# The last block pair of each FFN: left half of the down columns plain and joined with the lone block, right half by seven products

## The chip, the cores and the metric

The kernel runs on one core of one Trainium2 chip. The metric is the device time of one execution in microseconds (us). Before the change it is 2223.72 us, the median of three runs (2223.66 to 2224.74).

## The reference, cut to what matters

Two layers. Each has a mixer (not touched by the change) and ends with a SwiGLU FFN; the residual stream has 256 tokens of 2048 numbers, the FFN's hidden width is 5632, and everything is float32:

```python
        x = x + rms_norm(mix, g[1])
        h = rms_norm(x, g[2])
        f = (jax.nn.silu(h @ ffn_w_gate[layer]) * (h @ ffn_w_up[layer])) @ ffn_w_down[layer]
        x = x + rms_norm(f, g[3])
```

## The kernel before, in words

**Tiles.** The 256 tokens are two tiles of 128 (`t` = 0, 1). The hidden width is cut into 11 blocks of 512, the output width 2048 into 4 column blocks of 512 (`n` = 0 to 3). Weights come from memory in halves of 128x1024 numbers (512 KB). Every half is split into a rounded part `whi` (one copy on ACT, line 184) and a rest `wlo` (one subtraction on DVE, line 186), both kept in pools of seven buffers. A product with one 128x512 weight piece is three matmuls: high by `whi`, high by `wlo`, low by `whi` (lines 211 to 213 in `unit_a`, lines 618 to 620 in `quads`). A plain down product of one hidden block, one token tile and one column block is 4 pieces, so 12 matmuls.

**FFN.** `gate_up(b, ...)` makes the gate and up products of hidden block `b` by `unit_a` (8 chunks, 192 matmuls), forms `h` on DVE (line 466) out of the two accumulators and transposes it on PE (line 285, tile `tp`). Blocks 0 to 9 go in five pairs. After a pair, `combos` makes seven left operands `so` of the four transposed `h` tiles (ACT copy, DVE subtraction, and DVE sums), and `quads` runs as a generator in the background of the next pair's `gate_up`: for the left columns (`p` = 0: n = 0, 1) and then the right ones (`p` = 1: n = 2, 3) it makes the product of 2 hidden blocks, 2 token tiles and 2 column blocks by seven products in place of eight (84 matmuls in place of 96). The price is on DVE: 8 additions of weight halves (line 567, `sw<-sw,sw`), 14 splits in place of 8, and 10 additions of a product into the output sums `f` and a helper sum `fu` (line 627). Weights of `quads` come over a stream of their own into tiles `sw` (line 523).

**The lone block.** Block 10 has no pair. During its `gate_up` the quads of the last pair (blocks 8 and 9) run in the background: `tick` after every part of a unit adds `0.5 * rate` to a credit, and each whole credit advances the generator by one step; the rate is 1.0 in the pairs and 2.0 here. A quad has four steps of settling (once per pair) and 14 steps. What is left after the lone block's `gate_up` is run at once; then `fu` is added to or taken from `f` (lines 508 and 510), and `post` makes the lone block's own down products (one chunk of 12 matmuls per `n` and `t`, operands `hth`, `htl`), the norm of `f`, and the residual sum into `x`. `post` begins by loading the residual `x` again from memory (`load_x`, line 635, four transfers of 512 KB on POOL's queue) and the gains `gb` (line 371), before any of its products.

**Order.** The instruction order on each engine is made by a list scheduler from priorities; the engines then run their queues in order. In the FFN `tight` makes `unit_a` alternate the two token tiles; without it, the second token tile's parts lag by up to four (`push`). `wstream` and `sstream` (both on SP's queue) are packed in the order in which the program asks for weights.

Of the kernel before, what the change touches and what calls it, by code (L numbers as in the profile page):

```python
# [18 lines left out]
F32 = mybir.dt.float32  # L19
F32R = mybir.dt.float32r  # L20
# [6 lines left out]
P = 128  # L27
# [64 lines left out]
class Trunk:  # L92
# [102 lines left out]
        while self.pending:  # L195
            self.pending.popleft()()

    def unit_a(self, chunks, xk, evac):

        nc = self.nc  # L200
        last = len(chunks) - 1
        ps = {}

        def part(t, ci, w, kt0, half):
            if ci == 0 and half == 0:
                ps[t] = self.pacc.tile([P, 512], F32, tag="acc", name=self.nm("acc"))
            for k in (2 * half, 2 * half + 1):
                wh, wl = w[half]
                xh, xl = xk(kt0 + k, t)
                s, e = ci == 0 and k == 0, ci == last and k == 3  # L210
                self.pin(nc.tensor.matmul(ps[t], xh, wh[:, k % 2], start=s, stop=False))  # L211
                self.pin(nc.tensor.matmul(ps[t], xh, wl[:, k % 2], start=False, stop=False))  # L212
                self.pin(nc.tensor.matmul(ps[t], xl, wh[:, k % 2], start=False, stop=e))  # L213
# [132 lines left out]
        nc.vector.tensor_copy(row, ps)  # L346
        return row

    def post(self, li, gi, nseg, after, f=None):


        nc = self.nc
# [4 lines left out]
        rs = [self.small([P, 1], "prs", "prs") for _ in range(2)]  # L357
        state = {"si": 0}

        def seg(mk, xk):  # L360
            si = state["si"]
            state["si"] += 1
            last = si == nseg - 1
            if last:
                self.x = [[None, None], [None, None]]
                for t in range(2):
                    for j in range(2):
                        self.load_x(t, j, nc.gpsimd)
# [48 lines left out]
            for n in range(4):  # L417
                def evac(t, ps, n=n):
                    if not last:
                        return add(t, ps, n)  # L420
                    if n == 3 and t == 0:
                        self.prep()
                        self.pinning = ("PE", "DVE")
                    with self.tc.high_priority(offset=NORM):
                        d = add(t, ps, n, n == 3)
                        self.sumsq(d, ssp[t][:, n:n + 1])
                        if n == 3:
                            self.rstd(ssp[t], 4, D, rs[t])
                        i = (nc.gpsimd if n < 3 or (t and MULP and not (li == 1 and gi == 3)) else nc.vector).tensor_mul(out=d, in0=d, in1=gb[n])
                        if n == 3:  # L430
                            self.pin(i)
                    if n == 3 and t == 0:
                        self.pinning = ("PE",)
                        self.pending.popleft()()
                        self.pending.popleft()()
                        self.pinning = ("PE", "DVE")
                if last and n == 2:
                    self.pinned = {}
                    self.pinning = ("PE",)
                self.unit_a(mk(n), xk, evac)  # L440
            if last:
                run(PROG[0])
                assert not self.pending
# [8 lines left out]
    def ffn(self, li, norm, after):  # L452
        nc = self.nc
# [18 lines left out]
        f = [[self.slot([P, 1024], nm="f") for _ in range(2)] for _ in range(2)] + [self.slot([P, 1024], nm="fu")]  # L472
        self.rate, self.width = 1.0, 1
        for pi, pair in enumerate(PAIRS):
            self.squeue.extend((li, b, n) for p in range(2) for b, n in (
                (pair[0], 2 * p), (pair[0], 2 * p + 1), (pair[1], 2 * p + 1), (pair[1], 2 * p)))
        for pi, pair in enumerate(PAIRS):
            h = {}
# [10 lines left out]
            self.flush()  # L489
            while self.bg:  # L490
                self.step()
            self.spawn(self.quads(li, pair, self.combos(h), f, pi == 0))
        ht = self.new_xt(1, "ht")

        def whole(t, tp):
            sl = slice(t * P, (t + 1) * P)
            self.split(tp, ht[0][0][:, :, sl], ht[1][0][:, :, sl])
        self.rate = 2.0
        gate_up(LONE, whole)
        while self.bg:  # L500
            self.step()
        for n in range(4):
            u = f[2][:, n // 2 * 512:n // 2 * 512 + 512]
            c = slice(n % 2 * 512, n % 2 * 512 + 512)
            for t in range(2):
                d = f[t][n // 2][:, c]
                if n % 2 == 0 and t:
                    nc.vector.tensor_add(d, d, u)
                if n % 2:
                    nc.vector.tensor_sub(d, d, u)  # L510
        self.tight = False
        seg = self.post(li, 3, 1, after, f[:2])
        seg(lambda n: [("ffn_w_down", li, 512 * LONE, 512 * n, 0)], self.xk(ht))

    def sload(self):

# [8 lines left out]
        self.splan.append(("A", "ffn_w_down", li, 512 * b, 512 * n))  # L525
        self.sraw[li, b, n] = tiles

    def combos(self, h):

        nc = self.nc  # L530
        out = {}

        def put(key, src):
            o = self.slot([P, 2, 4, P], F32R, "so")
            nc.scalar.copy(o[:, 0], src)
            nc.vector.tensor_sub(o[:, 1], src, o[:, 0].bitcast(F32))  # L536
            out[key] = o
        put("b11", h[0, 0])
        put("b21", h[0, 1])
        put("t4", h[1, 1])  # L540
# [14 lines left out]
    def quads(self, li, pair, ops, f, first):  # L555

        nc = self.nc
        for _ in range(SETTLE):
            yield
        for p in range(2):  # L560
            n0, n1 = 2 * p, 2 * p + 1
            raw = {}

# [45 lines left out]
            for key in order:  # L609
                ps = self.mx([P, 512], "sq")  # L610
                x = ops[key]
                for i in range(2):
                    next(ahead, None)
                    wh, wl = (v.rearrange("p (k n) -> p k n", k=2) for v in ready.popleft())
                    for k in range(2):
                        s, e = i == 0 and k == 0, i == 1 and k == 1
                        xh, xl = x[:, 0, 2 * i + k], x[:, 1, 2 * i + k]
                        nc.tensor.matmul(ps, xh, wh[:, k], start=s, stop=False)  # L618
                        nc.tensor.matmul(ps, xh, wl[:, k], start=False, stop=False)  # L619
                        nc.tensor.matmul(ps, xl, wh[:, k], start=False, stop=e)  # L620
# [790 lines left out]
```

## Time and profile before

| what | value |
|---|---|
| median of three runs | 2223.72 us |
| the profiled execution | 2221.77 us |
| its span, first to last instruction | 2220.0 us |
| PE busy | 2173.3 us (98%) |
| PE weight loads busy | 1829.0 us (82%) |
| DVE busy | 1772.4 us (80%) |
| ACT busy | 1213.5 us (55%) |
| mean granted TensorE clock | 0.992 |

The profiled execution took 1.77 us more than its span and 1.95 us less than the median. Each row of the profile's groups gives a line, an engine, an operation with its output and inputs, the count, the busy time and the mean duration in ns. Matmuls overlap in PE's pipeline, so a row's duration of 0.39 us is longer than the distance between two starts; where PE's pace is wanted, starts are compared.

### The profile page before, as it was taken

Reading aid. Unit: us, or ns where it says so; the run is one execution under the profiler, and the core shown is the slowest. Engines: PE = TensorE matmul, PEld = TensorE weight load, DVE = VectorE, ACT = ScalarE, POOL = GpSimd, SP = SyncE. Lnnn points to the kernel's source line nnn. Section 1 sums busy time; section 2 is a strip of 40 time slices with the busy share of each in tenths; the row PEclk is TensorE's granted clock in tenths of the full one; section 3 lists DMA queues with packets and bytes.
Section 4 is the critical chain, followed back from the end, with each engine's and each line's share of the span. In section 5 each row is a group of like instructions: output and inputs, shape, how many; then the busy total and the mean of one; then the engine's idle time right before and its main releaser. Section 6 shows DMA issues by size and latency. Waiting matters only on the chain.

```text
span 2220.0 us, 28963 instructions
## 1 busy us (share of the span) xinstructions
PE 2173.3 (98%) x10840; PEld 1829.0 (82%) x10840; DVE 1772.4 (80%) x2137; ACT 1213.5 (55%) x1515; POOL 205.3 (9%) x246
## 2 busy tenths in 40 slices
PE   8999999999999999999989999999999999999997
PEld 7989998788888888888768988878888888888875
DVE  7987545766878898888989988676687889888896
ACT  7544435555565555555656545655555555555563
POOL 0001010210000000000021362121000000000002
PEclk9999999999999999999999999999999999999998
DMA  8445565574665555465556443657466555646563
GB/s 282 133 133 184 182 203 182 180 258 157 204 234 189 204 178 201 159 217 199 204 188 223 158 144 114 224 187 260 158 201 229 198 204 170 202 165 209 199 216 116
DMA packets 117325, 424.54 MB, mean 191 GB/s; under 512 B 13392, under 2 KB 13520, under 8 KB 117184
## 3 DMA queue, kind: packets, MB, share of 16 engines
q1 hardware_dynamic: 110592, 400.61, 53.6%
q0 software_dynamic: 6448, 21.99, 3.0%
q8 instruction: 85, 1.39, 0.2%
q14 instruction: 56, 0.46, 0.1%
q10 hardware_dynamic: 144, 0.10, 0.0%
HBM read 414.25 MB, written 8.39 MB: 190 GB/s over the span
## 4 chain that ended last, share of the span: by engine, by line
PE 86%; DVE 10%; issue 2%; POOL 1%; DMA 1%; ACT 0%; DVEq 0%; POOLq 0%; ACTq 0%
PE acc L213 19%; PE acc L212 19%; PE acc L211 19%; DVE wlo L186 5%; PE sq L618 5%; PE sq L619 5%; PE sq L620 5%; PE accb L242 3%; PE accb L244 3%; PE accb L243 3%; PE tp L285 1%; DVE sw L567 1%; DVE xtl L331 1%; DVE f L627 1%; PE gs L819 1%
## 5 line engine op out<-in xcount | busy, mean ns | idle before, releaser
L186 DVE TENSOR_TENSOR wlo<-raw,whi 128x1024 fp32r<-128x1024 f32 x596 | 740.0, 1249 | 278.0 <-ACT whi L184 270.7
L184 ACT CAST whi<-raw 128x1024 fp32r<-128x1024 f32 x596 | 624.7, 1052 | 572.1 <-PE acc L213 388.7
L213 PE MATMUL acc<-whi,xtl 128*128 128x512 f32 x1760 | 689.7, 393 | 5.9 <-DVE xtl L331 5.9
L212 PE MATMUL acc<-wlo,xth 128*128 128x512 f32 x1760 | 689.3, 393 | 0.8 <-DVE wlo L186 0.8
L211 PE MATMUL acc<-whi,xth 128*128 128x512 f32 x1760 | 677.4, 393 | 3.1 <-ACT xth L328 3.0
L184 ACT CAST whi<-sw 128x1024 fp32r<-128x1024 f32 x280 | 293.7, 1054 | 232.0 <-PE acc L213 131.0
L213 PEld LDWEIGHTS acc<-whi,xtl 128*128 128x128 f32 x1760 | 332.4, 189 | 78.1 <-DVE xtl L331 9.3
L211 PEld LDWEIGHTS acc<-whi,xth 128*128 128x128 f32 x1760 | 332.3, 189 | 73.0 <-ACT xth L328 5.1
L212 PEld LDWEIGHTS acc<-wlo,xth 128*128 128x128 f32 x1760 | 332.4, 189 | 70.4 <-DVE wlo L186 1.7
L186 DVE TENSOR_TENSOR wlo<-sw,whi 128x1024 fp32r<-128x1024 f32 x280 | 338.2, 1222 | 48.9 <-ACT whi L184 46.0
L619 PE MATMUL sq<-wlo,so 128*128 128x512 f32 x560 | 220.0, 393 | 4.5 <-DVE wlo L186 4.5
L620 PE MATMUL sq<-whi,so 128*128 128x512 f32 x560 | 219.4, 392 | 0.0
L618 PE MATMUL sq<-whi,so 128*128 128x512 f32 x560 | 219.0, 393 | 0.0
L567 DVE TENSOR_TENSOR sw<-sw,sw 128x1024 f32<-128x1024 f32 x160 | 194.1, 1221 | 16.8 <-DMA sw<-sstream 16.3
L242 PE MATMUL accb<-xth,whi 128*128 128x256 f32 x608 | 173.8, 286 | 0.0
L244 PE MATMUL accb<-xth,wlo 128*128 128x256 f32 x608 | 173.0, 284 | 0.0
L243 PE MATMUL accb<-xtl,whi 128*128 128x256 f32 x608 | 172.7, 284 | 0.0
L619 PEld LDWEIGHTS sq<-wlo,so 128*128 128x128 f32 x560 | 105.9, 189 | 28.5 <-DVE wlo L186 7.0
L620 PEld LDWEIGHTS sq<-whi,so 128*128 128x128 f32 x560 | 106.0, 189 | 22.5 <-DVE so L536 0.6
L618 PEld LDWEIGHTS sq<-whi,so 128*128 128x128 f32 x560 | 105.8, 189 | 22.1 <-ACT whi L184 0.4
L635 POOL DMA_DIRECT2D x<-xm x8 | 4.4, 546 | 1292.5 <-ACT whi L184 645.6
L242 PEld LDWEIGHTS accb<-xth,whi 128*128 128x128 f32 x608 | 116.5, 192 | 1.4 <-issue 0.7
(248 smaller groups left out, 2226.9 us busy)
## 6 DMA issues: line engine op xcount, KB each, us to landing
raw<-wstream SPq DMA_DIRECT2D x596, 512.0 KB, 4.9
sw<-sstream SPq DMA_DIRECT2D x160, 512.0 KB, 6.2
gb<-norm_gains POOLq DMA_DIRECT2D x16, 256.0 KB, 7.6
xm<-x POOLq DMA_DIRECT2D x16, 256.0 KB, 3.5
x<-xm POOLq DMA_DIRECT2D x8, 512.0 KB, 5.1
x<-x SPq DMA_DIRECT2D x4, 512.0 KB, 8.2
x<-x POOLq DMA_DIRECT2D x4, 512.0 KB, 7.8
xf<-x POOLq DMA_DIRECT2D x8, 256.0 KB, 3.4
```

Source lines behind the costliest of these rows:

```text
L184: self.pin(nc.scalar.copy(hi, src))
L186: self.pin(nc.vector.tensor_sub(lo, src, hi.bitcast(F32)))
L211: self.pin(nc.tensor.matmul(ps[t], xh, wh[:, k % 2], start=s, stop=False))
L212: self.pin(nc.tensor.matmul(ps[t], xh, wl[:, k % 2], start=False, stop=False))
L213: self.pin(nc.tensor.matmul(ps[t], xl, wh[:, k % 2], start=False, stop=e))
L242: nc.tensor.matmul(ps, wh[:, kt % 8], xh, start=kt == 0, stop=False)
L243: nc.tensor.matmul(ps, wh[:, kt % 8], xl, start=False, stop=False)
L244: nc.tensor.matmul(ps, wl[:, kt % 8], xh, start=False, stop=kt == 15)
L567: nc.vector.tensor_add(a, a, b)
L618: nc.tensor.matmul(ps, xh, wh[:, k], start=s, stop=False)
L619: nc.tensor.matmul(ps, xh, wl[:, k], start=False, stop=False)
L620: nc.tensor.matmul(ps, xl, wh[:, k], start=False, stop=e)
```

## The change

The last pair's left columns leave `quads` (`COLS`). Their products go into `unit_a` together with the lone block's: for n = 0 and 1 a unit has three chunks (blocks 8, 9 and 10), for n = 2 and 3 one. The pair's operands come from `combos`, which already has three of the four plain ones (`b11`, `b21`, `t4`) and now makes the fourth, `a21`, for this pair. The background rate during the lone block is 0.75 in place of 2.0, so that the remaining quad runs on into the units n = 0 and 1 and is drained ahead of n = 2. These two units are tight, but for the last chunk of n = 1. The helper sum `fu` is taken in at n = 0 for the left columns and at n = 2 for the right ones, and the residual `x` is loaded at n = 2.

```diff
-NCHUNK = 298
-NQUAD = 80
+COLS = [(0, 1)] * 4 + [(1,)]
+NCHUNK = 306
+NQUAD = 72
+ENDRATE = .75
...
-            if self.tight:
+            if self.tight and (loose is None or ci < loose):
...
+        def reload():
+            self.x = [[None, None], [None, None]]
+            for t in range(2):
+                for j in range(2):
+                    self.load_x(t, j, nc.gpsimd)
...
             if last:
-                self.x = [[None, None], [None, None]]
-                for t in range(2):
-                    for j in range(2):
-                        self.load_x(t, j, nc.gpsimd)
+                if before is None:
+                    reload()
...
+                if before is not None:
+                    before(n)
+                    if n == 2:
+                        reload()
...
-                self.unit_a(mk(n), xk, evac)
+                self.unit_a(mk(n), xk, evac, len(mk(n)) - 1 if n == 1 else None)
...
-            self.spawn(self.quads(li, pair, self.combos(h), f, pi == 0))
+            ops = self.combos(h, pi == len(PAIRS) - 1)
+            self.spawn(self.quads(li, pair, COLS[pi], ops, f, pi == 0))
...
-        self.rate = 2.0
+        def before(n):
+
+            if n == 2:
+                while self.bg:
+                    self.step()
+                self.tight = False
+            if n % 2 == 0:
+                u = f[2][:, n // 2 * 512:n // 2 * 512 + 512]
+                left, right = ([f[t][n // 2][:, c * 512:c * 512 + 512] for t in range(2)] for c in range(2))
+                nc.vector.tensor_add(left[1], left[1], u)
+                for d in right:
+                    nc.vector.tensor_sub(d, d, u)
+
+        def operand(kt, t):
+            b, k = kt // 4, kt % 4
+            if b == 2:
+                return self.xk(ht)(k, t)
+            o = ops[(("b11", "a21"), ("b21", "t4"))[b][t]]
+            return o[0][:, k], o[1][:, k]
+        self.rate = ENDRATE
         gate_up(LONE, whole)
-        while self.bg:
-            self.step()
...
-        seg(lambda n: [("ffn_w_down", li, 512 * LONE, 512 * n, 0)], self.xk(ht))
+        own = [(b, 4 * i) for i, b in enumerate((*PAIRS[-1], LONE))]
+        seg(lambda n: [("ffn_w_down", li, 512 * b, 512 * n, k) for b, k in (own[2:] if n > 1 else own)], operand)
...
+        if whole:
+            out["a21"] = self.mtmp([P, 4, P], F32R, "a21"), self.mtmp([P, 4, P], F32R, "a21")
+            part("a21", h[1, 0])
...
-        for p in range(2):
+        for p in cols:
```

Over both layers PE gets 24 instructions more (10522 to 10546), DVE 46 fewer (2139 to 2093) and ACT 10 fewer (1418 to 1408); SP's loads stay 756 in number and alike in size (16 of `sw` become 16 of `raw`).

Three places in the first layer. **PE, at the end of the lone block's up product** (`acc_9373` and `acc_9236` are its last accumulators; `tp` with `h` is the transpose of the lone block's hidden tile; `sq` is the quad). Before:

```order
L211 MATMUL acc_9373<-whi_9610,xth_4217 128x512
L212 MATMUL acc_9373<-wlo_9612,xth_4217 128x512
L213 MATMUL acc_9373<-whi_9610,xtl_4218 128x512
L285 MATMUL tp_9658<-ca,h_9656 128x128 x4
L618 MATMUL sq_9665<-whi_9623,so_9005 128x512
L619 MATMUL sq_9665<-wlo_9625,so_9005 128x512
```

The same place now:

```order
L216 MATMUL acc_9236<-whi_9388,xtl_4218 128x512
L646 MATMUL sq_9404<-whi_9359,so_9020 128x512
...
L214 MATMUL acc_9483<-whi_9473,so_8999 128x512
...
L215 MATMUL acc_9490<-wlo_9475,a_1785_9028 128x512
...
L216 MATMUL acc_9483<-whi_9479,so_8999 128x512
L288 MATMUL tp_9423<-ca,h_9421 128x128 x4
L288 MATMUL tp_9438<-ca,h_9436 128x128 x4
```

The transposes stood right behind the up product's last matmul; now 6 matmuls of the quad and 15 of the pair's plain products (`acc_9483`, `acc_9490`) stand between.

**DVE, at the same point** (`h_9656` and `h_9421` are the lone block's hidden tiles of t = 0). Before:

```order
L627 TENSOR_TENSOR f_4270<-f_4270,sq_9620 128x512
L186 TENSOR_TENSOR wlo_9753<-raw_9608,whi_9751 128x1024
L510 TENSOR_TENSOR f_4272<-f_4272,fu_4273 128x512
L186 TENSOR_TENSOR wlo_9759<-raw_9720,whi_9757 128x1024
L466 SCALAR_TENSOR_TENSOR h_9656<-acc_9359,nrs_4144,sg_9305 128x512
L466 SCALAR_TENSOR_TENSOR h_9678<-acc_9373,nrs_4300,sg_9330 128x512
```

Now:

```order
L188 TENSOR_TENSOR wlo_9475<-raw_9335,whi_9473 128x1024
L188 TENSOR_TENSOR wlo_9481<-raw_9380,whi_9479 128x1024
L188 TENSOR_TENSOR wlo_9506<-sw_9363,whi_9504 128x1024
L477 SCALAR_TENSOR_TENSOR h_9421<-acc_9229,nrs_4144,sg_9195 128x512
L477 SCALAR_TENSOR_TENSOR h_9436<-acc_9236,nrs_4300,sg_9203 128x512
```

From the last pair's last `h` of t = 0 up to and with the lone block's first `h`, DVE's queue held 97 instructions, 59 of 128x1024 and 38 of 128x512; now it holds 52, 32 and 20.

**POOL, the reload of x** (`gb` are the gains, `f_4269` with `gb_9714` or `gb_9462` is the product for n = 1, t = 0, `prs` the norm's factor). Before:

```order
L635 DMA x_9704<-xm_147 128x1024
L635 DMA x_9706<-xm_147 128x1024
L635 DMA x_9708<-xm_148 128x1024
L635 DMA x_9710<-xm_148 128x1024
L371 DMA gb_9712<-norm_gains 128x512
L371 DMA gb_9714<-norm_gains 128x512
L371 DMA gb_9716<-norm_gains 128x512
L371 DMA gb_9718<-norm_gains 128x512
L429 TENSOR_TENSOR f_4269<-f_4269,gb_9712 128x512
L429 TENSOR_TENSOR f_4269<-f_4269,gb_9714 128x512
```

Now:

```order
L378 DMA gb_9464<-norm_gains 128x512
L378 DMA gb_9466<-norm_gains 128x512
L436 TENSOR_TENSOR f_4269<-f_4269,gb_9460 128x512
L436 TENSOR_TENSOR f_4271<-f_4271,gb_9460 128x512
L436 TENSOR_TENSOR f_4269<-f_4269,gb_9462 128x512
L663 DMA x_9755<-xm_147 128x1024
L663 DMA x_9757<-xm_147 128x1024
L663 DMA x_9759<-xm_148 128x1024
L663 DMA x_9761<-xm_148 128x1024
L436 TENSOR_TENSOR f_4270<-f_4270,gb_9464 128x512
L302 TENSOR_TENSOR prs_9458<-ms_9828,mhalf 128x1
```

The four loads of `x` moved behind the gains' loads and three multiplications, to just ahead of the multiplication for n = 2.

More of the change, by code (lines that the diff above doesn't have):

```diff
@@ L347, in rstd_rows, with post @@
         return row
-    def post(self, li, gi, nseg, after, f=None):
+    def post(self, li, gi, nseg, after, f=None, before=None):
         nc = self.nc
@@ L474, in ffn @@
         for pi, pair in enumerate(PAIRS):
-            self.squeue.extend((li, b, n) for p in range(2) for b, n in (
+            self.squeue.extend((li, b, n) for p in COLS[pi] for b, n in (
                 (pair[0], 2 * p), (pair[0], 2 * p + 1), (pair[1], 2 * p + 1), (pair[1], 2 * p)))
@@ L497, in whole @@
             self.split(tp, ht[0][0][:, :, sl], ht[1][0][:, :, sl])
-        self.rate = 2.0
-        gate_up(LONE, whole)
-        while self.bg:
-            self.step()
[L502 to L512, printed above, removed]
-        seg(lambda n: [("ffn_w_down", li, 512 * LONE, 512 * n, 0)], self.xk(ht))
+        def before(n):
[16 more added lines that the diff above has]
+        self.rate = ENDRATE
+        gate_up(LONE, whole)
+        seg = self.post(li, 3, 1, after, f[:2], before)
+        own = [(b, 4 * i) for i, b in enumerate((*PAIRS[-1], LONE))]
+        seg(lambda n: [("ffn_w_down", li, 512 * b, 512 * n, k) for b, k in (own[2:] if n > 1 else own)], operand)
     def sload(self):
@@ L534, in put, with part @@
             o = self.slot([P, 2, 4, P], F32R, "so")
-            nc.scalar.copy(o[:, 0], src)
-            nc.vector.tensor_sub(o[:, 1], src, o[:, 0].bitcast(F32))
-            out[key] = o
+            out[key] = o[:, 0], o[:, 1]
+            part(key, src)
+        def part(key, src):
+            hi, lo = out[key]
+            nc.scalar.copy(hi, src)
+            nc.vector.tensor_sub(lo, src, hi.bitcast(F32))
         put("b11", h[0, 0])
```

8 lines of the change are left out of this document (4 added, 4 removed).

## The prediction

> **What bounds the kernel now.** First the page's first part, the busy time of each engine:
>
> ```profile
> span 2220.0 us, 28963 instructions
> PE 2173.3 (98%) x10840; PEld 1829.0 (82%) x10840; DVE 1772.4 (80%) x2137; ACT 1213.5 (55%) x1515; POOL 205.3 (9%) x246
> ```
>
> PE bounds the whole, so 24 more matmuls look like a loss. But these are averages over stages. So next the busy time in four stretches: the lone block's stage in the two layers, then the pairs ahead of it (us, then busy time and count by engine, then the granted clock).
>
> ```profile
> 1040.00:1135.00 95.00, 89.22 (x383) 72.05 (x382) 93.13 (x101) 51.73 (x57) 4.30 (x8) 0.96 0.55 186
> 2093.00:2187.00 94.00, 87.25 (x380) 69.98 (x379) 91.86 (x100) 51.25 (x57) 4.30 (x8) 0.98 0.52 174
> 575.00:1035.00 460.00, 460.00 (x2060) 381.54 (x2059) 389.86 (x390) 259.29 (x275) 0.00 (x0) 1.00 0.59 202
> 1670.00:2090.00 420.00, 420.00 (x1878) 348.22 (x1877) 357.42 (x361) 236.44 (x251) 0.00 (x0) 1.00 0.60 205
> ```
>
> In the pairs PE never stops (460.00 of 460.00) and DVE is 85% busy. In the lone block's stage it is the other way round: DVE is busy 98% of the time and PE falls behind. PE's pace in the pairs is 460 / 2060 = 0.2233 us for an instruction. At that pace 95 us would hold 425 and 94 us would hold 421; there are 383 and 380. So 42 x 0.2233 + 41 x 0.2233 = 9.5 + 9.1 = 18.6 us of PE's time is lost in these two stages. The waits of PE in (nearly) the same windows say for whom:
>
> ```profile
> PE tp L285 <- DVE h L466: 3.5, 1, 3.5
> PE sq L619 <- DVE wlo L186: 2.3, 2, 1.8
> ...
> PE tp L285 <- DVE h L466: 3.9, 1, 3.9
> PE sq L619 <- DVE wlo L186: 2.2, 2, 1.8
> PE acc L212 <- DVE wlo L186: 0.6, 1, 0.6
> ```
>
> All on DVE, 5.8 + 6.7 = 12.5 us. The other 6 us lie in what follows a wait. PE's timeline around one (start, duration, and in brackets the idle time):
>
> ```profile
> 1092.40 0.39 PE L618 MATMUL sq<-whi,so 128*128 128x512 f32 x1
> 1094.60 0.50 PE L619 MATMUL sq<-wlo,so 128*128 128x512 f32 x1 [1.81 <-DVE wlo L186]
> ...
> 1095.26 0.63 PE L618 MATMUL sq<-whi,so 128*128 128x512 f32 x1
> ...
> 1098.24 0.50 PE L213 MATMUL acc<-whi,xtl 128*128 128x512 f32 x1
> 1098.58 0.39 PE L212 MATMUL acc<-wlo,xth 128*128 128x512 f32 x1
> 1098.81 0.40 PE L213 MATMUL acc<-whi,xtl 128*128 128x512 f32 x1
> ```
>
> From 1095.26 to 1098.24 seven matmuls start 0.43 us apart, then again 0.23: a wait also costs some us at half pace, about 1.5 here. The longest wait, in the second layer, first on PE, then DVE's queue during it:
>
> ```profile
> 2176.56 0.39 PE L213 MATMUL acc<-whi,xtl 128*128 128x512 f32 x1
> 2180.86 1.12 PE L285 MATMUL tp<-ca,h 128*128 128x128 f32 x4 [3.91 <-DVE h L466]
> ```
>
> ```profile
> 2176.58 0.69 DVE L627 TENSOR_TENSOR f<-f,sq 128x512 f32<-128x512 f32 x1
> 2177.18 1.23 DVE L186 TENSOR_TENSOR wlo<-raw,whi 128x1024 fp32r<-128x1024 f32 x1
> 2178.32 0.69 DVE L510 TENSOR_TENSOR f<-f,fu 128x512 f32<-128x512 f32 x1
> 2178.92 1.23 DVE L186 TENSOR_TENSOR wlo<-raw,whi 128x1024 fp32r<-128x1024 f32 x1
> 2180.05 1.41 DVE L466 SCALAR_TENSOR_TENSOR h<-acc,nrs,sg 128x512 f32<-128x512 f32 x2
> ```
>
> DVE works without a break: `h` needs nothing but its turn. It is backlog, not a dependency. That decides the case: backlog goes away if DVE has less to do.
>
> **Part by part.** *PE's new work.* One quad in each layer becomes plain: 96 - 84 = 12 matmuls, 24 in all, on the path, 24 x 0.2233 = 5.4 us (5.5 at the timeline's 0.23). Weight loads stay beneath: 1829.0 / 10840 = 0.17 us each.
>
> *DVE's saving.* DVE's groups in the first layer's stage, 1038 to 1131 us:
>
> ```profile
> L186 DVE TENSOR_TENSOR wlo<-sw,whi 128x1024 fp32r<-128x1024 f32 x27 | 32.2, 1227 | 0.0
> L186 DVE TENSOR_TENSOR wlo<-raw,whi 128x1024 fp32r<-128x1024 f32 x17 | 20.4, 1230 | 0.0
> L567 DVE TENSOR_TENSOR sw<-sw,sw 128x1024 f32<-128x1024 f32 x16 | 19.3, 1225 | 0.0
> L627 DVE TENSOR_TENSOR f<-f,sq 128x512 f32<-128x512 f32 x16 | 10.5, 690 | 0.0
> L466 DVE SCALAR_TENSOR_TENSOR h<-acc,nrs,sg 128x512 f32<-128x512 f32 x4 | 2.9, 753 | 0.0
> L536 DVE TENSOR_TENSOR so<-sd,so 128x512 fp32r<-128x512 f32 x4 | 2.7, 690 | 0.0
> ```
>
> In each layer 8 additions of weights (9.8 us), 14 - 8 = 6 splits (7.3) and 10 additions of products (6.9) go, and one operand split for `a21` comes (0.7): 23.3 us less. It does not come off the time; it only ends waits.
>
> *Does the backlog end?* The order gives DVE's queue from the last pair's last `h` to the lone block's first: 59 long and 38 short instructions before, 32 and 20 now. In the timeline long ones start 1.14 us apart (2177.18 to 2178.32) and short ones 0.60 (2176.58 to 2177.18). Before that makes 59 x 1.14 + 38 x 0.60 = 90 us, which is the whole stage of 93 us: a stage paced by DVE. Now it makes 36.5 + 12 = 48.5 us. PE's queue over the same stretch now holds 240 matmuls up to the transposes of the lone block, 240 x 0.2233 = 53.6 us. DVE has 5 us to spare, and starts ahead of PE by what it led with when the stage began. So I take it that DVE keeps up, and the waits on `wlo` and `h` as they stand go, with their half pace: -18.6 us. If only the idle time came back and something else kept the slow pace, it would be -12.5.
>
> A rule bears on this split. The Trainium skill, TensorE: Matmul & The Clock Gate, What's actually happening, has the array's clock fall to half after an idle window of about 3.4 us and rise after as long a busy one. The 0.43 us spacing agrees with half; that it came after a gap of 1.81 us does not. By the rule alone only the waits of 3.5 and 3.9 us cause half pace, the 1.5 us at 1095 would stay, and the sum below would be 1.5 us smaller.
>
> *What is late next.* The lone block's `h` is no longer behind a backlog but behind one split that waits for a buffer: `wlo_9506` takes over the pool's buffer seven back, which the quad's last matmul ahead of the plain products reads. From there ACT copies, DVE subtracts and `h` follows: ACT's copy takes as long as DVE's split or less (1213.5 us for 1515 instructions is 0.80 in the mean), so at most 1.23 + 1.23 + 0.75 = 3.2 us and three handovers. PE has 15 plain matmuls, 3.3 us, as cover. So the transposes are nearly in time, the second `h` 0.6 to 0.7 behind: I leave 0.7 us in each layer, +1.4 (bounds 0 and 2 x 2).
>
> *Moves with one answer.* `fu` goes into `f` by the same 6 DVE instructions, elsewhere in a queue that now has room. `a21` adds one copy on ACT, at 55%. The weights' bytes and loads are the same. Left-out lag in the units n = 0, 1 changes only the order of PE's matmuls, and all their operands but the lone chunk's exist.
>
> *The reload of x.* It moves on POOL's queue from ahead of the gains to behind the multiplication for n = 1, t = 0. The rows that bound it: an addition of n = 1 with its POOL multiplication, then the last addition before the norm and the first use of x; last the landings of a 512 KB load of x on POOL's queue.
>
> ```profile
> 1139.30 0.69 DVE L381 TENSOR_TENSOR f<-f,acc 128x512 f32<-128x512 f32 x1 [1.58 <-PE acc L213]
> 1147.17 0.68 DVE L381 TENSOR_TENSOR f<-f,acc 128x512 f32<-128x512 f32 x1
> 1150.41 1.76 DVE L413 SCALAR_TENSOR_TENSOR x<-f,prs,x 128x512 f32<-128x512 f32 x2
> ```
>
> ```profile
> 1140.88 1.29 POOL L429 TENSOR_TENSOR f<-f,gb 128x512 f32<-128x512 f32 x1 [1.03 <-ACT sq L303]
> ```
>
> ```profile
> x<-xm POOLq DMA_DIRECT2D x8, 512.0 KB, 5.1
> x<-x POOLq DMA_DIRECT2D x4, 512.0 KB, 7.8
> ```
>
> From the addition for n = 1 (1139.30) to the end of its multiplication (1142.17) is 2.9 us; then the first load goes out and lands 5.1 us later, at 8.0. The first use comes 24 matmuls (5.4 us) and 3.2 us (1147.17 to 1150.41) after the same addition, at 8.6. So it lands 0.6 us early; at 7.8 us it lands 2.1 late, 4.2 us in two layers. Nothing is queued behind these issues on POOL that is due before. I take 0, and 4.2 as an end.
>
> **Sum.** +5.4 - 18.6 + 1.4 = -11.8 us. The profiled execution's 2221.77 becomes 2210.0; the median stands 1.95 us above it, so 2223.72 - 11.8 = 2211.9, rounded to 2212. All PE's loss back and no residue gives 2210.5; the waits alone gives 2223.72 + 5.4 - 12.5 + 1.4 = 2218.0.
>
> **The rivals.**
>
> *PE adds, the waits stay (slower).* If the waits were dependencies, they would follow PE's matmuls: +5.4 us, 2229.1. It decides this way if DVE's 48.5 us before the lone block's `h` grew beyond PE's 53.6, or if `h` waited for its buffer longer than the 15 matmuls cover. For it: PE at 98%. Against it: DVE's unbroken queue during the 3.9 us. The Trainium skill says to optimise the most-contended engine first (Perfetto Trace Analysis, Identifying the Most-Contended Engine); by that rule alone this is the outcome, and the stretches above disagree with it for this stage. 5%.
>
> *x lands late.* Should the loads land as late as 9.5 us after issue (by the 7.8 us row and some queueing), PE stands 4 us twice and 1.5 us twice at half pace: 2211.9 + 11 = 2223, no change. For it: loads of weights share the engines of the transfers, and the margin is 0.6 us. Against it: 5.1 us is the row of these very tiles. 6%.
>
> *Half of the waits return*, as smaller ones: at the pair's operand sums, where 11 short DVE instructions and ACT copies feed each other, or with x 2.1 us late: 2216 (2214.5 to 2218). 15%.
>
> *The tail gains too*, since DVE and POOL arrive at the norm with an empty queue: 2207.5. 4%.
>
> **How the numbers follow.** 70% for 2212 (2209 to 2214.5); with the half case and the tail the range is 2207.5 to 2218. A measurement here tells about 0.2%, 4.4 us, from no change, so faster means under 2219.3: 0.70 + 0.15 + 0.04 = 0.89. Within: 0.06. Slower: 0.05.
>
> **What would show it.** In the changed kernel the waits of PE on `h` and `wlo` in the lone block's stages should be under 1 us each; DVE should show idle time there; matmuls 0.23 us apart all through; `tp<-ca,h` for the lone block without a 3.5 us gap; the first use of x not ended by a DMA. Wrong would be a wait on `wlo` in the units n = 0, 1, a wait of DVE's line 420 for x's DMA, or a DVE still busy over 95% up to the lone `h`.

## The result and the profile after

The changed kernel takes 2207.18 us, the median of four runs (2206.36 to 2209.29); the kernel before, run beside it, 2224.15 us (2223.66 to 2224.74). The ratio is 0.9925, with a 95% interval of 0.9908 to 0.9942: faster by 17.0 us. The forecast was 2212.0 us, in a range from 2207.5 to 2218.0. The direction and the mechanism held, but the gain came out 4.8 us larger, and the time lies 0.3 us below the range: the forecast of the size failed. The profiled execution after took 2206.36 us, its span 2204.6 us.

First the busy time of each engine over the whole span of the changed kernel, as in the prediction's first fence:

```profile
span 2204.6 us, 28951 instructions
PE 2169.5 (98%) x10864; PEld 1831.1 (83%) x10864; DVE 1733.7 (79%) x2091; ACT 1204.5 (55%) x1505; POOL 207.7 (9%) x246
```

This line hardly differs from that of before: PE stands at 98% again, with 24 instructions more. It would not have told that the kernel got faster, nor why. The stretches do. These are the lone block's stage in the two layers, then the first layer's pairs ahead of it (us; busy time and count of PE, of its weight loads, of DVE, ACT and POOL; granted clock, share and rate of the transfers):

```profile
1040.00:1128.00 88.00, 88.00 (x398) 73.03 (x398) 74.21 (x78) 48.97 (x57) 5.81 (x6) 1.00 0.51 171
2085.00:2171.00 86.00, 86.00 (x389) 71.41 (x388) 72.55 (x76) 47.62 (x56) 5.81 (x6) 1.00 0.49 165
575.00:1035.00 460.00, 460.00 (x2059) 381.58 (x2058) 392.04 (x394) 258.51 (x274) 0.00 (x0) 1.00 0.59 202
```

In the first two rows PE is now busy from end to end (88.00 of 88.00, 86.00 of 86.00) at a granted clock of 1.00, and DVE, at 98% before, is busy for 74.21 of 88 us, 84%. The stage looks like the pairs in the row below. The waits of PE over the whole span, in full, have nothing left on `h` or `wlo` in these stages:

```profile
PE acc L216 <- DVE xtl L334: 7.5, 8, 1.9
PE tp L288 <- DMA ca<-ca: 5.0, 1, 5.0
PE tp L288 <- DVE x L420: 3.5, 4, 1.4
PE acc L214 <- ACT xth L331: 3.1, 4, 1.4
PE yp L1273 <- POOL seg L1267: 2.3, 2, 1.5
PE tp L288 <- PE acc L216: 0.8, 2, 0.4
PE tp L288 <- POOL x L418: 0.6, 1, 0.6
```

Then the lone block's hidden tile. On DVE's timeline (start, duration, idle time in brackets) it is the last row; on PE's below it stand the quad's last matmul, the first and the last plain one and the transposes `tp`:

```profile
1091.42 1.23 DVE L188 TENSOR_TENSOR wlo<-raw,whi 128x1024 fp32r<-128x1024 f32 x1 [1.50 <-ACT whi L186]
1092.78 1.23 DVE L188 TENSOR_TENSOR wlo<-sw,whi 128x1024 fp32r<-128x1024 f32 x1
1093.93 1.40 DVE L477 SCALAR_TENSOR_TENSOR h<-acc,nrs,sg 128x512 f32<-128x512 f32 x2
```

```profile
1095.35 0.39 PE L648 MATMUL sq<-whi,so 128*128 128x512 f32 x1
1095.58 0.39 PE L214 MATMUL acc<-whi,so 128*128 128x512 f32 x1
...
1098.75 0.40 PE L216 MATMUL acc<-whi,so 128*128 128x512 f32 x1
1098.99 1.03 PE L288 MATMUL tp<-ca,h 128*128 128x128 f32 x8
```

DVE has a break here (1.50 us, waiting for ACT's copy); both hidden tiles are done at 1095.33, 3.7 us before PE comes to transpose them.

Where the time went, from one mark to the next on PE's timeline (us; the marks are the first transpose of the last pair's `h`, 1042.86 before and 1043.69 after in the first layer, and the first transpose of the next norm's `x`):

| stretch | before | after | difference |
|---|---|---|---|
| start to the last pair's `h`, layer 0 | 1042.86 | 1043.69 | +0.8 |
| from there to the next norm, layer 0 | 108.70 | 100.95 | -7.8 |
| from there to the first `h` of layer 1 | 386.89 | 386.12 | -0.8 |
| on to the last pair's `h`, layer 1 | 557.36 | 557.16 | -0.2 |
| from there to PE's last instruction | 111.77 | 104.24 | -7.5 |
| what follows PE's last instruction | 12.42 | 12.42 | 0 |

The sum is -15.4 us, 2221.77 to 2206.36. The other 1.6 us of the medians' 17.0 is which runs were profiled: the one of before lies 2.4 us below its median, the one of after 0.8 below. A second profiled execution of the changed kernel (the last experiment) tells how firm these rows are. It has 100.96 and 104.24 us again in the two stages, but 387.53 in the stretch that follows the first of them, 1.4 more than the execution in the table. And in the kernel before and the three made from it below, the first mark lies between 1042.86 and 1044.59 us. So the two rows of -7.8 and -7.5 are the change; the other three are no larger than what differs from run to run.

### The profile page after: what moved, and what is told of

Read it like the earlier page. It is cut to its first block, busy times and chain, and to the rows that moved or that the text cites. A ratio compares the mean times of both kernels' runs of the same rounds, so it can differ in the third digit from the quotient of the medians.

```text
span 2204.6 us, 28951 instructions
## 1 busy us (share of the span) xinstructions
PE 2169.5 (98%) x10864; PEld 1831.1 (83%) x10864; DVE 1733.7 (79%) x2091; ACT 1204.5 (55%) x1505; POOL 207.7 (9%) x246
## 4 chain that ended last, share of the span: by engine, by line
PE 94%; DVE 4%; issue 1%; POOL 1%; DMA 0%; ACT 0%; DVEq 0%; POOLq 0%; ACTq 0%
PE acc L216 21%; PE acc L215 21%; PE acc L214 21%; PE sq L647 5%; PE sq L648 5%; PE sq L646 5%; PE accb L245 3%; PE accb L247 3%; PE accb L246 3%; DVE wlo L188 1%; PE tp L288 1%; DVE xtl L334 1%; PE gs L847 1%; PE as L981 1%; DVE x L420 1%
## 5 line engine op out<-in xcount | busy, mean ns | idle before, releaser
L188 DVE TENSOR_TENSOR wlo<-raw,whi 128x1024 fp32r<-128x1024 f32 x612 | 760.4, 1249 | 290.3 <-ACT whi L186 281.9
L186 ACT CAST whi<-raw 128x1024 fp32r<-128x1024 f32 x612 | 641.9, 1052 | 605.7 <-PE acc L216 419.6
L215 PEld LDWEIGHTS acc<-wlo,xth 128*128 128x128 f32 x1760 | 331.9, 189 | 68.8 <-DVE wlo L188 0.9
L186 ACT CAST whi<-sw 128x1024 fp32r<-128x1024 f32 x252 | 265.8, 1055 | 207.7 <-PE acc L216 138.4
L188 DVE TENSOR_TENSOR wlo<-sw,whi 128x1024 fp32r<-128x1024 f32 x252 | 305.4, 1221 | 54.7 <-ACT whi L186 51.6
L647 PE MATMUL sq<-wlo,so 128*128 128x512 f32 x504 | 196.1, 389 | 0.0
L648 PE MATMUL sq<-whi,so 128*128 128x512 f32 x504 | 196.1, 389 | 0.0
L646 PE MATMUL sq<-whi,so 128*128 128x512 f32 x504 | 195.8, 390 | 0.0
L595 DVE TENSOR_TENSOR sw<-sw,sw 128x1024 f32<-128x1024 f32 x144 | 174.6, 1220 | 16.3 <-DMA sw<-sstream 15.7
L247 PEld LDWEIGHTS accb<-xth,wlo 128*128 128x128 f32 x608 | 116.5, 192 | 1.4 <-issue 1.0
L246 PEld LDWEIGHTS accb<-xtl,whi 128*128 128x128 f32 x608 | 116.5, 192 | 0.6
L648 PEld LDWEIGHTS sq<-whi,so 128*128 128x128 f32 x504 | 94.6, 188 | 19.6
```

The costliest lines, as they stand in the source:

```text
L186: self.pin(nc.scalar.copy(hi, src))
L188: self.pin(nc.vector.tensor_sub(lo, src, hi.bitcast(F32)))
L246: nc.tensor.matmul(ps, wh[:, kt % 8], xl, start=False, stop=False)
L247: nc.tensor.matmul(ps, wl[:, kt % 8], xh, start=False, stop=kt == 15)
L595: nc.vector.tensor_add(a, a, b)
```

## The experiments

Two theories were set against each other. A: what counts is DVE's backlog, the work in its queue ahead of the lone block's hidden tile. B: what counts is the cover, the plain products that now stand ahead of the transposes on PE. Later a third was added, C: the lower background rate alone does it. In these runs the kernel before had medians of 2224.9 to 2225.1 us, and the ratios are to it.

**Take only DVE's work away.** The kernel before, without the last pair's 16 weight additions in each layer (line 567), so that its quads use the weights unsummed. There are no plain products, and the rate is the old one. The scheduler makes the order anew, and PE's matmuls change places from the stage's start on, but 156 of the quads' matmuls still stand between the last pair's transposes and the lone block's, as before.

```diff
             def add(dst, src):
+                if pair == PAIRS[-1]:
+                    return
```

> The kernel before, with the 16 additions of weight halves (sw<-sw,sw) of each layer's last pair left out; the products then use unsummed weights. PE's 84 matmuls in each quad, the order of the blocks, the rate and the place of the reload stay as before. Theory A (DVE's backlog is the cause): DVE's queue up to the lone block's h loses 16 x 1.14 = 18 us of 90 in a stage that takes PE about 84 us without waits, so the waits on wlo and h go nearly whole: 2224 - 17 = 2207 (2204 to 2211), the wait on h under 1.5 us. Theory B (what helps is the pair's plain products standing between the up product and the transposes, and the new order): h stands where it stood, its wait of 3.5 and 3.9 us stays, 2218 to 2224.

Measured: 2204.53 us (2204.08 to 2206.09), ratio 0.9909 [0.9893, 0.9926]. In the two stages' rows PE is busy nearly throughout, at full clock, with DVE at 78.50 of 88 and 76.70 of 86 us:

```profile
1040.00:1128.00 88.00, 87.28 (x393) 72.05 (x393) 78.50 (x88) 54.73 (x58) 4.30 (x8) 1.00 0.60 204
2085.00:2171.00 86.00, 85.28 (x384) 70.42 (x383) 76.70 (x85) 53.66 (x57) 4.30 (x8) 1.00 0.56 191
```

Relief for DVE alone brings all of the gain, 20.4 us, without any cover. That is A, and B falls as the main cause. It also shows the price of the change's way: it stands 2.7 us above. One thing goes besides DVE's time: ACT's copies no longer wait for a sum. That the amount of work counts by itself is the next run's part.

**Give DVE work back.** The changed kernel with additions that nobody uses, behind the splits of the lone block's `gate_up`: first 39 in each layer (24 of them between the two `h`, 14.4 us), then 13 (11 between them, 6.6 us).

```diff
+            if self.extra:
+                self.nextra += 1
+                for _ in range(self.extra[self.nextra % 2]):
...
+                    nc.vector.tensor_add(j, part, part)
...
+        self.extra = (1, 2)
         gate_up(LONE, whole)
+        self.extra = ()
```

> The changed kernel with idle work on DVE: during the lone block's gate and up products 39 additions of 128x512 in each layer into a scrap tile, each behind a split; 24 of them stand between the last pair's h and the lone block's h, 24 x 0.60 = 14 us. Theory A: DVE's 48.5 us in that stretch become 63, PE's are 53.6 with some 5 us of lead, so PE waits 4 to 8 us in each layer and loses some more at half pace: 2207 + 8 to 18 = 2215 to 2225. Theory B: DVE's load does not matter while the order is the new one: within 2 us of 2207.

> As the run with 39 additions, but with 13 in each layer, 11 of them between the two h: 6.6 us. Theory A: 48.5 + 6.6 = 55 us is covered by 53.6 and the lead: 2207 to 2210. Theory B: 2207. It places the point from which DVE decides.

Measured: with 39, 2225.76 us (2221.62 to 2226.61), ratio 1.0002 [0.9992, 1.0011], the whole gain gone and 0.8 us above A's range; with 13, `(0, 1)` in place of `(1, 2)`, 2207.62 us (2207.05 to 2208.86), ratio 0.9923 [0.9908, 0.9938], none of it gone. The waits of PE in the run with 39, in the first and then the second layer's stage:

```profile
PE acc L222 <- DVE wlo L189: 4.5, 1, 4.5
PE tp L295 <- DVE h L484: 1.7, 1, 1.7
...
PE acc L222 <- DVE wlo L189: 2.9, 1, 2.9
PE tp L295 <- DVE h L484: 1.7, 1, 1.7
```

They are again on `wlo` and `h`: the waits come back with the load. From mark to mark the two stages are 8.1 and 6.0 us longer than in the changed kernel, so 14.1 of the 15.3 us that they had gained are gone; the rest of the run's loss lies outside them. The order did not stay quite the same: with 39 the scheduler put the transposes ahead of the quad's and the plain matmuls, so the waits of 1.7 us on `h` may owe to the missing cover; those on `wlo`, inside the lone block's `gate_up`, do not. DVE's room in the stage lies between 13 such additions and 39 (6.6 and 14.4 us ahead of the lone `h`). In the first layer's longest wait a part is a transfer: DVE stood 3.1 us for a load of `sw`, after which the split came late. That load went out at 1078.55 us (in the changed kernel at 1072.42), behind loads into `raw` that waited on SP's queue for DVE's splits, so it was late with DVE.

**Take the cover away.** The changed kernel with the lone block's chunk first in the units n = 0 and 1, and the pair's plain chunks behind it, so that the transposes follow the quad's matmuls at once.

```diff
-... (own[2:] if n > 1 else own)], operand)
+... (own[2:] if n > 1 else own[2:] + own[:2])], operand)
```

> The changed kernel with the lone block's chunk first in the units n = 0 and 1, the pair's two behind it: the transposes lose the 15 plain matmuls that stood ahead of them. Theory A: without a backlog h comes about 2 us after the up product's last matmul, and 6 matmuls of the quad are still ahead: 1 to 4 us in each layer at most, 2209 to 2214. Theory B: the cover was the gain, the waits of 3.5 and 3.9 us and their half pace return: 2216 to 2222.

Measured: 2207.98 us (2206.77 to 2210.72), ratio 0.9926 [0.9911, 0.9940], below A's range of 2209 to 2214 too. On DVE's and PE's timelines:

```profile
1094.67 1.40 DVE L477 SCALAR_TENSOR_TENSOR h<-acc,nrs,sg 128x512 f32<-128x512 f32 x2
```

```profile
1096.09 0.40 PE L648 MATMUL sq<-whi,so 128*128 128x512 f32 x1
1096.32 1.04 PE L288 MATMUL tp<-ca,h 128*128 128x128 f32 x8
```

`h` is done at 1096.07 and transposed at 1096.32, without a gap. The 15 plain matmuls ahead of the transposes were worth under 1 us: from mark to mark the stages take 101.01 and 104.30 us, against 100.95 and 104.24.

**The price of the matmuls.** The changed kernel with 12 matmuls made twice in each layer, in block 4's gate product, where PE does not wait.

```diff
...
+                for k in (0, 1):
+                    for wk in (w[0][0], w[0][1], w[0][0]):
+                        self.pin(nc.tensor.matmul(ps[t], xk(kt0 + k, t)[0], wk[:, k], ...))
```

> The changed kernel with 12 more matmuls in each layer, repeats inside one unit of block 4's gate product, where PE does not wait; the output differs by these repeats. It measures the term of the added matmuls by itself. If 24 more matmuls cost PE's pace, 24 x 0.2233 = 5.4 us over the changed kernel's 2207.2: 2212.6 (2211.5 to 2213.7). If such matmuls were hidden beneath something: 2207 to 2209.

Measured: 2212.77 us (2211.79 to 2215.64), ratio 0.9946 [0.9932, 0.9961]; 5.6 us above the changed kernel, where 5.4 was the term. In the traces the stretch with the repeats, from one block's transposes to the next, takes 63.49 and 63.46 us in the two layers, where the changed kernel takes 60.74 in both: 5.5 us. PE does not wait in the pairs, and each added instruction came at its full price.

**The rate.** First the changed kernel with the old rate, then the kernel before with a lower one.

```diff
-ENDRATE = .75
+ENDRATE = 2.0
```

> The changed kernel with the old background rate 2.0 during the lone block in place of 0.75. DVE's and PE's work is the same as in the changed kernel; the quad is run earlier. Theory A (less work for DVE is what counts): DVE still has 5 us or more to spare by the lone block's hidden tile, and the quad's 84 matmuls stand ahead of the transposes as well: 2206 to 2211. Theory C (the spreading by the lower rate is what counts): the waits of before come back, 2214 to 2222.

```diff
-        self.rate = 2.0
+        self.rate = 1.0
```

> The kernel before with the background rate 1.0 during the lone block in place of 2.0, so that part of the two quads' work falls behind the lone block's hidden tile; all work stays. Theory A: DVE's sum of work over the stage is the same and there are no plain products to hold beside it, so the loss moves to behind the hidden tile: 2218 to 2224. Theory C (the lower rate alone takes the waits away): 2206 to 2212.

Measured: the changed kernel at rate 2.0, 2215.67 us (2215.40 to 2215.78), ratio 0.9957 [0.9942, 0.9972]. The kernel before at rate 1.0, 2221.53 us (2218.99 to 2223.13), ratio 0.9986 [0.9976, 0.9995].

| | old rate 2.0 | lower rate |
|---|---|---|
| both halves by seven products | 2224.9 | 2221.5 (1.0) |
| left half plain | 2215.7 | 2207.2 (0.75) |

The first run lies in C's range and above A's, but without the waits of before that C had expected; the second lies in A's range and far above C's. So neither theory has both. By the medians about half of the gain needs the lower rate. The stage of the first layer in halves of 40 us shows why, first of the changed kernel at rate 2.0:

```profile
1045.00:1085.00 40.00, 38.43 (x170) 30.56 (x169) 39.27 (x45) 26.18 (x31) 2.20 (x4) 1.00 0.34 108
1085.00:1125.00 40.00, 40.00 (x182) 33.18 (x181) 27.14 (x28) 16.95 (x19) 0.00 (x0) 1.00 0.73 248
```

and of the changed kernel as it is:

```profile
1045.00:1085.00 40.00, 40.00 (x178) 33.12 (x177) 37.09 (x41) 22.60 (x27) 2.20 (x4) 1.00 0.46 157
1085.00:1125.00 40.00, 40.00 (x182) 33.23 (x181) 31.71 (x33) 21.31 (x24) 3.62 (x2) 1.00 0.53 171
```

DVE has nearly the same work in both, 66.4 and 68.8 us in 80. At rate 2.0 it is crowded into the first half (39.27 of 40 us), where PE waits again, and DVE is idle for a third of the second. The waits of PE in that stage:

```profile
PE sq L647 <- DVE wlo L188: 1.1, 2, 0.6
PE sq L648 <- DVE so L562: 0.5, 1, 0.5
```

From the last pair's `h` to the next norm, or to PE's end, it takes 103.66 and 106.95 us against 100.95 and 104.24, so 5.4 us of the 8.5 lie in the two stages, a third of the 15.3 that they had gained. Of the 9.0 us between the two profiled runs, 2.8 lie in the second layer's mixer (the last section) and 1.1 ahead of the first stage, where the rate is the same; those are not shown to be the rate's. In the kernel before, the lower rate has no work beside which it could spread the surplus. Its waits of PE over the whole span:

```profile
PE sq L619 <- DVE wlo L186: 6.9, 10, 1.6
...
PE tp L285 <- DVE h L466: 2.5, 2, 1.2
```

The wait on `h` has shrunk to 1.2 us in each layer, but ten waits on `wlo` stand ahead of quad matmuls. So for this change less work for DVE and an even spread are both needed. It is the spread that counts, and not a low rate as such: the kernel without the weight additions kept rate 2.0, had two quads to run with it, and was even by itself (DVE 36.60 and 35.06 us in the same two halves).

**Move the sums to POOL.** An attempt at a faster kernel: that of before, but with the last pair's weight additions on POOL, which is at 9%.

```diff
-                        nc.vector.tensor_add(a, a, b)
+                        (nc.gpsimd if pair == PAIRS[-1] else nc.vector).tensor_add(out=a, in0=a, in1=b)
```

> The kernel before, with all seven-product columns kept, but the last pair's 16 sums of weight halves per layer are made on POOL in place of DVE. PE's work stays at 10522 instructions. Theory A (DVE's backlog): DVE loses 16 x 1.14 = 18 us of queue per layer ahead of the lone block's hidden tile, as in the run that left the sums out (2204.5 us), so 2203 to 2209, with PE waits on h and wlo gone. POOL's multiplication of 128x512 took 1.29 us, so a sum of 128x1024 is put at 2.6 us and 16 of them at 42 of 93 us. Theory B (the cover, plain products ahead of the transposes): no plain products there, so 2218 to 2224. Rival for POOL: its sums come late or slow DVE down, then waits on sw or wlo stand in place of the old ones: 2210 to 2220.

Measured: 2248.76 us (2248.25 to 2249.36), ratio 1.0106 [1.0091, 1.0121], slower than everything else and outside all three ranges; the rival for POOL named what happened, but not its size. The groups of POOL, DVE and ACT in the first layer's stage (count, then busy time and mean ns, then the engine's idle time before them and what ended it):

```profile
L567 POOL TENSOR_TENSOR sw<-sw,sw 128x1024 f32<-128x1024 f32 x15 | 51.5, 3459 | 26.8 <-DVE wlo L186 15.8 <-DMA sw<-sstream 10.9
L186 DVE TENSOR_TENSOR wlo<-sw,whi 128x1024 fp32r<-128x1024 f32 x26 | 40.1, 1569 | 7.7 <-ACT whi L184 7.7
L186 DVE TENSOR_TENSOR wlo<-raw,whi 128x1024 fp32r<-128x1024 f32 x16 | 23.2, 1485 | 0.0
L627 DVE TENSOR_TENSOR f<-f,sq 128x512 f32<-128x512 f32 x15 | 9.8, 676 | 0.0
L184 ACT CAST whi<-sw 128x1024 fp32r<-128x1024 f32 x25 | 25.7, 1051 | 33.3 <-POOL sw L567 26.0 <-DMA sw<-sstream 2.9 <-PE sq L620 2.8
```

and POOL's timeline with DVE's beside it:

```profile
1041.12 12.22 POOL L567 TENSOR_TENSOR sw<-sw,sw 128x1024 f32<-128x1024 f32 x4
```

```profile
1048.18 2.89 DVE L536 TENSOR_TENSOR so<-hT,so 128x512 fp32r<-128x512 f32 x1
1051.00 2.88 DVE L545 TENSOR_TENSOR sd<-sd,hT 128x512 f32<-128x512 f32 x1
1053.81 0.68 DVE L536 TENSOR_TENSOR so<-hT,so 128x512 fp32r<-128x512 f32 x1
```

POOL's four additions end at 1053.34 us. The first two DVE rows, beside them, take 2.9 us; the third, just behind them, takes 0.68. So work moved to POOL came back as longer work on DVE. And the sums took 3.5 us each in the mean, so that ACT's copies waited 26.0 us for them and the splits behind came late. No kernel of these runs that does all of the reference's work was faster than the changed one.

**The reload of x.** The stretch from the norm of layer 0 to layer 1 had come out 0.8 us shorter in the first profiled run, which the prediction had at nothing. The changed kernel with the loads of `x` at the segment's start, and the changed kernel beside it:

```diff
-                if before is None:
-                    reload()
+                reload()
...
-                    if n == 2:
-                        reload()
```

> The changed kernel with the residual x loaded again at the start of the lone block's segment, as before the change, in place of at n = 2. The stretch from the FFN of the first layer to the mixer of the second came out 0.8 to 0.9 us shorter in the changed kernel's trace, which the prediction had at nothing. If the later loads cause that, 0.8 to 1.8 us (one or two layers) over the changed kernel of the same batch. If the place of the loads is worth nothing: the same within 0.8 us, and the 0.9 us has to come from what PE and DVE do there.

> The changed kernel itself once more, on the same chip as the run with the early loads of x, as its measure: 2206.4 to 2209.3 as before.

Measured: 2209.47 us (2208.40 to 2210.14) against 2207.21 (2206.38 to 2207.80), ratios to before 0.9930 [0.9916, 0.9944] and 0.9919 [0.9906, 0.9933]. The medians differ by 2.3 us, more than the 0.8 to 1.8 expected, but the two intervals overlap and the traces give the loads less. In the traces the norm's transposes of `x` take 31.38 us from first to last with the early loads and 30.40 with the late ones (30.43 in the second execution, 31.42 in the kernel before). The last row of each fence is where the norm's next step can start, on DVE's timeline with the early loads, then with the late ones:

```profile
1146.46 5.74 DVE L188 TENSOR_TENSOR wlo<-raw,whi 128x1024 fp32r<-128x1024 f32 x2
1152.12 0.74 DVE L419 SCALAR_TENSOR_TENSOR x<-f,prs,x 128x512 f32<-128x512 f32 x1
```

```profile
1143.52 1.69 DVE L420 SCALAR_TENSOR_TENSOR x<-f,prs,x 128x512 f32<-128x512 f32 x2
1145.13 4.78 DVE L188 TENSOR_TENSOR wlo<-raw,whi 128x1024 fp32r<-128x1024 f32 x2
1149.83 0.74 DVE L420 SCALAR_TENSOR_TENSOR x<-f,prs,x 128x512 f32<-128x512 f32 x1
```

The same two splits take 5.74 and 4.78 us, and POOL is at work on `f` and `x` beside both. That the place of POOL's instructions makes the 1 us is argued from this and from the run with the sums on POOL, not shown; the kernel before at rate 1.0 has the early loads too and takes 30.60. The other 1.3 us of the medians are not shown to be the loads': in the traces 1.3 us stand ahead of the last pair of layer 0 (1045.02 against 1043.72 us), which these loads do not touch.

## Why the cause was right and the size wrong

The cause that the prediction named is the one that the runs show: DVE's backlog in two stages. The time fell out of the range because of three terms. The loss that goes was put at 18.6 us and measured 20.7. The residue of 1.4 us rested on a wait that was not there. And the moved loads of `x` were costed as 0 or a loss, while the norm behind them came out some 1 us shorter.

*PE's new work, +5.4.* Right: 5.6 us by the medians of the repeated matmuls, 5.5 by the traces.

*DVE's backlog is what PE waits for.* Right, by the runs that take load away and give it back. The queue up to the lone `h` was put at 48.5 us; the two stretches of 55 us from transpose to transpose show 49.42 and 49.27, with 52 instructions each:

```profile
1044.00:1099.00 55.00, 49.42 (x52) 1.00 0.48 163
2088.00:2143.00 55.00, 49.27 (x52) 1.00 0.48 162
```

The saving of 23.3 us in each layer, which enters no sum, was too large: it adds up durations, and these overlap. With the prediction's own distances of 1.14 and 0.60 us the 14 long and 9 short instructions make 21.4, and DVE's busy time fell by 19.4 us in each layer (1772.4 to 1733.7 for the two together).

*The loss that goes, -18.6.* The mechanism was right, the term too small: this is the largest of the three failures. The stages gained 7.75 + 7.53 = 15.3 us with 5.4 us of work added, so 20.7 us of loss went. The prediction read the term with the pairs' pace, 0.2233 us for an instruction. The changed kernel without waits goes through these stages at 88.00 / 398 = 0.2211; at that pace the prediction's two windows had lost 10.3 + 10.0 = 20.3 us. The alternative of 12.5 us, the waits alone, is excluded: the half pace went as well. The term also rests on the rate, which the prediction didn't name: 5.4 us of it come back at rate 2.0. The rate was inside the count of 52 instructions only by the order that it made. Of the 45 instructions by which DVE's queue ahead of the lone `h` got shorter (97 to 52), 23 are gone from the layer; the other 22 only moved behind it.

*What is late next, +1.4.* This step failed. The prediction said that the split `wlo_9506` ahead of `h` waits for a buffer which the quad's last matmul reads, so that 15 matmuls are all the cover. The timeline above has that split (`wlo<-sw`) at 1092.78 and the quad's last matmul at 1095.35: it cannot have waited for it. ACT's copy for this split did wait for a matmul of the quad, but for one that started at 1091.27, 18 matmuls earlier:

```profile
1091.69 1.06 ACT L186 CAST whi<-sw 128x1024 fp32r<-128x1024 f32 x1 [0.30 <-PE sq L648]
```

So the prediction had picked the wrong reader of the buffer. `h` was 3.7 us early, and in the run with the lone chunk first it needed no cover at all. The residue was nothing.

*The reload of x, 0.* The loads landed in time, as the margin of 0.6 us had it. POOL's issues:

```profile
1136.34 1.29 POOL L436 TENSOR_TENSOR f<-f,gb 128x512 f32<-128x512 f32 x1 [13.55 <-ACT sq L306]
1137.57 2.15 POOL L663 DMA_DIRECT2D x<-xm  x4
```

The four loads landed between 1142.85 and 1146.60 us, and DVE's first use started at 1143.52, 0.67 after the first landing and without a wait. But the step failed in that it was costed on one side only: 0 to +4.2. No reason excluded a gain, and with the late loads the norm's transposes took 1.0 us less in the traces (0.8 over the whole stretch in the first profiled run). What makes that 1 us stays open. The range needed an end below for it.

*The sum.* -11.8 was forecast. The loss is 2.1 larger, the residue of 1.4 is not there, the stretch with the norm gives 0.8, the start of this run took 0.8 more, the pairs of layer 1 0.2 less: -15.5, against -15.4 measured between the two profiled runs. The three failed terms alone make -16.1, so 2207.6 from the median of before, 0.4 above what was measured. The range's low end, 2207.5, was that of the rival with a faster tail; a loss larger than 18.6 us and a norm that gains had no place in it, and both came. That the measured time stands next to that rival's is chance.

*The rivals.* PE's added work with the waits kept (2229.1) did not happen. The rule of the Trainium skill named there, taken over the whole span, would have spoken against a change that is right: for PE the section goes by the weight loads' busy share (and by a measure that no run here gives), 82% before and 83% after, above DVE's 80 and 79%, and the gain lay in a stage of each layer that DVE paced. x landing late did not happen. Half of the waits did not return; a time like that came up only at the old rate, by another cause (2215.7, where the rival stood at 2216). What follows PE's last instruction gained nothing, 12.42 us in both.

## What to carry to other kernels

Read the stage, not the span: an engine at 98% of the whole can still lose 20 us in two stages that another engine paces. Giving the bound engine 5 us more work paid here because it took some 20 us in each layer off the engine that it waits for, and it paid fully only with what is left spread evenly over the stage. Cost a moved transfer on both sides. And an engine at 9% is not free help: here POOL's additions made DVE's own work longer.

## What the runs showed of the hardware

**A POOL addition holds up DVE.** Beside POOL's additions a DVE addition of 128x512 out of SBUF took 2.88 us in place of 0.68, while `f<-f,sq`, which reads one operand from PSUM, kept its 676 ns (six of the 15 ran wholly beside a POOL addition, at 0.67 to 0.68 us). The Trainium skill, SBUF — State Buffer, SBUF: two separate sides, describes a pair of ports that a DVE instruction with two SBUF inputs and a POOL instruction that reads SBUF hold in turn, each for its whole length. The traces agree: POOL's additions take 3.1 us each (12.22 for four), and the DVE additions beside them start 2.8 us apart.

**The same wait costs half pace in one place and not in another.** Two stretches of 10 us in the kernel before, each with a PE wait of 1.81 us on `wlo`, first in layer 0, then in layer 1:

```profile
1090.00:1100.00 10.00, 8.19 (x29) 5.97 (x28) 10.00 (x11) 3.11 (x4) 0.00 (x0) 0.83 0.46 156
...
2143.00:2153.00 10.00, 8.19 (x35) 6.07 (x35) 10.00 (x11) 3.13 (x4) 0.00 (x0) 1.00 0.49 164
```

The first has a granted clock of 0.83 and 29 matmuls, the second 1.00 and 35. In the second layer's mixer PE waits 1.48 and 0.83 us for POOL's `seg` in both of the next runs. In the changed kernel's profiled run the clock stayed at 1.00 behind it; in that of rate 2.0 it was 0.77 over 15 us, with 13 matmuls fewer. From the norm's last transpose of `x` to the mixer's first of `y` it took 232.0 us in the one and 234.8 in the other, and 233.6 in the second execution of the changed kernel:

```profile
1296.00:1311.00 15.00, 12.69 (x66) 10.40 (x65) 11.49 (x23) 6.02 (x8) 11.06 (x12) 1.00 0.34 103
```

```profile
1300.00:1315.00 15.00, 12.69 (x53) 10.41 (x52) 9.51 (x17) 4.40 (x5) 9.96 (x11) 0.77 0.20 63
```

The Trainium skill, TensorE: Matmul & The Clock Gate, What's actually happening, calls the window in which the activity is measured free-running, so that the place of a gap in it varies from run to run. That fits the difference. Its table lets the clock fall after an idle window of about 3.4 us; that does not fit half pace behind a gap of 1.81 us, and here the measurement decides. For a comparison of two kernels it means that up to 2.8 us in an untouched stage need be no effect of the change.
